# Feed-forward up and down products of a hybrid RWKV-7/S5 layer written out as one ordered pipeline on four queues

## Chip, cores and metric

The kernel runs on one core of a Trainium2 chip. The metric is the device time of one execution in microseconds (us); the time before is the median of three runs. The traces are taken by the hardware profiler from one further execution. PE is TensorE, DVE VectorE, ACT ScalarE, POOL GpSimd, and SP SyncE, which here only issues transfers; ACT issues transfers too.

## The reference, cut to what matters

One layer: RMSNorm, two token mixers in parallel (RWKV-7 and S5), output projection and residual; then the part that is changed here, and a final RMSNorm. Everything is float32.

```python
D_MODEL = 1024; BATCH = 1; SEQ = 1024; DEPTH = 1; D_FF = 4 * D_MODEL
def sq_relu_mlp(x, w_up, w_down):
    return jnp.square(jax.nn.relu(x @ w_up)) @ w_down
...
    x = x + (g_a * y_a + g_b * y_b) @ w_out[l]
    x = x + sq_relu_mlp(rmsnorm(x, norm2_g[l]), w_ff_up[l], w_ff_down[l])
return rmsnorm(x, norm_f_g)
```

## The kernel before

**Precision.** Each float32 operand is split into a high part `hi` (a rounded copy that ACT makes, L123) and a low part `lo = src - hi` (DVE, L117). A product of two operands is three matmuls: hi x hi, hi x lo, lo x hi.

**Strassen.** Both feed-forward matrices are multiplied as 2 x 2 blocks in seven products P1 to P7 (the Winograd form) instead of eight. Each product multiplies a weight block or a sum of weight blocks by a moving block or a sum of moving blocks; `MOV` names the moving one ("11", "21", "22", T1 to T4). Sums of products give the four blocks of the result.

**The up product** (hidden = relu(...)^2, 4096 channels by 1024 tokens) runs in 16 pairs `Pair(j)`, two in each of eight rounds, a (even j) and b (odd j). A pair's product is 12 matmuls of 128 x 512: 4 blocks along the contraction, 3 matmuls each (L1096 to L1098). `w[n]()` returns the split weights of product n; `ready_w` makes them at the first call: P5 needs one sum of weight blocks before (`s1`), P6 three (`s2_`), the others none. The methods P1, P5, P6 run the product and copy its bank out on ACT (tiles `d`, `v5`, `u2`), P2 with C11, P3 and P7 add such a copy to a bank on DVE (`tt`), then `hidden` scales and clips it on DVE (`stt`, L120) and squares it on ACT; P4 does the last two. P1, P6, P7 and P4 of one pair use one bank `x`, P5 and P3 a bank `z`, P2 a bank `y`. Round 0 has the statistics of the second RMSNorm in its midst (`norm_stat`, `norm_out`), which give the scales `rs`.

`moving` then makes the sums T1, T2, T3, T4 of the four hidden blocks on DVE and writes the seven moving blocks to the scratch `tD` in memory, seven issues of 256 KB on ACT's queue (L1208). The w_up weights of a pair come in four loads per round, 512 KB each, on SP's queue (L1066).

**The down product** runs its seven products in the order P1, P5, P6, P7, P3, P2, P4, each over eight units q. `unit(n, q)` loads a 512 KB block of w_dn and a 512 KB block of `tD` (tile `traw`, L1298), forms the weight sum in the kept blocks on DVE, and splits both into `rb` tiles (`rhi`, `rlo`); a unit is 24 matmuls (L1305 to L1307). After a product, DVE adds its four banks to the residual tiles `x2`, loaded within P1. The last two units of P4 are cut into 256-column pieces, with the final norm between them.

**Room.** `gp` has 32 slots of 128 x 512; fourteen of them hold the split moving operands with k = 3 all through the up product, the others rotate for weights and T1, T2, T4. The other split moving operands lie in the pools kxa and kxb (tiles `kx`), which later hold kept weight blocks of the down product. `rb` opens where `gp` closes, 16 slots, of which nine are first taken by unused tiles `rskip`.

**What sets the order.** Every engine runs its own instructions in one order. Only in the last pieces are PE and DVE taken as written (`tc.manual_schedule(engines={E.PE, E.DVE})`); everywhere else the framework's scheduler orders the instructions of each engine from data dependences and modelled times. Transfers signal their landing on eight semaphores in rotation (DMAHW0 to DMAHW7); the next user of a semaphore waits for the transfer that used it before.

## Time and profile before

| quantity | value |
| --- | --- |
| time before, median of 3 | 1618.44 us (1617.98 to 1620.98) |
| profiled execution | 1623.29 us |
| its span, first to last instruction | 1621.5 us |
| PE busy | 94% |
| DVE busy | 66% |
| ACT busy | 45% |
| mean granted clock of TensorE | 0.966 |
| HBM traffic over the span | 142 GB/s |

Times in the profile are in us from the span's start. A row of a timeline gives start, duration, engine (with a q behind it: its queue, issuing a transfer), line, operation, output<-input, shape, count, and in brackets the idle time before and what ended it. L12 is line 12 of the kernel that the row is from. Matmul durations overlap, since matmuls are pipelined: how far starts lie apart is what one costs. The clock is in shares of the full TensorE clock.

### The profile page before, as it was taken

The numbers are of one execution on the slowest core, as the hardware profiler recorded it, in microseconds if no ns is written. First come the engines' busy times: TensorE is split into PE (matmuls) and PEld (weight loads), VectorE is DVE, ScalarE is ACT, GpSimd is POOL, SyncE is SP. The second block draws the span as 40 slices with busy tenths as digits, with TensorE's granted clock in tenths as the row PEclk, the third lists the DMA queues.
The fourth block names the chain that finished last, engine by engine and source line by source line (L and its number), as shares of the span: only waits on it lengthen the run. The fifth ranks groups of instructions, "written<-read, shape, count | busy, mean of one in ns | idle before, by whom it ended". The sixth has DMA issues, their size and how long they took to land.

```text
span 1621.5 us, 22364 instructions
## 1 busy us (share of the span) xinstructions
PE 1529.1 (94%) x8056; PEld 1240.7 (77%) x8056; DVE 1077.0 (66%) x2119; ACT 730.1 (45%) x1259; POOL 80.2 (5%) x107
## 2 busy tenths in 40 slices
PE   7999999999999999999999888889888699999997
PEld 5787787787788778788888776667676578888886
DVE  8668767877576778656666655655655578756564
ACT  7645566765664443234444433323333244333441
POOL 3110001011011010000000000000000000000000
PEclk9999899999999999999999998989989899999998
DMA  7544434245335245741244323332324966532571
GB/s 236 182 146 134 127 105 131 86 143 151 92 117 172 77 132 164 253 124 46 78 149 156 122 102 127 122 138 110 108 100 176 348 222 197 192 104 91 182 245 54
DMA packets 137679, 232.73 MB, mean 144 GB/s; under 512 B 42529, under 2 KB 52897, under 8 KB 137569
## 3 DMA queue, kind: packets, MB, share of 16 engines
q1 hardware_dynamic: 119648, 195.65, 37.7%
q10 hardware_dynamic: 17280, 33.56, 5.4%
q0 software_dynamic: 640, 2.10, 0.6%
q8 instruction: 63, 1.03, 0.3%
q14 instruction: 48, 0.39, 0.1%
HBM read 167.16 MB, written 62.91 MB: 142 GB/s over the span
## 4 chain that ended last, share of the span: by engine, by line
PE 85%; DVE 5%; DMA 4%; ACT 3%; issue 1%; SPq 1%; ACTq 0%; POOL 0%; POOLq 0%; DVEq 0%
PE mm L162 6%; PE mm L160 6%; PE mm L161 6%; PE b L160 4%; PE b L162 4%; PE b L161 4%; PE mm L1096 4%; PE mm L1097 4%; PE mm L1098 4%; PE b L1306 4%; PE b L1307 4%; PE b L1305 3%; PE b L1096 2%; PE b L1097 2%; PE sm L718 2%; PE b L1098 2%
## 5 line engine op out<-in xcount | busy, mean ns | idle before, releaser
L160 PE MATMUL mm<-s,whi 128*128 128x512 f32 x528 | 213.6, 405 | 0.0
L162 PE MATMUL mm<-s,wlo 128*128 128x512 f32 x528 | 213.3, 404 | 0.0
L161 PE MATMUL mm<-s,whi 128*128 128x512 f32 x528 | 210.6, 399 | 0.0
L123 ACT ACTIVATE whi<-wraw 128x512 fp32r<-128x512 f32 x176 | 103.2, 624 | 149.4 <-PE mm L161 54.4
L117 DVE TENSOR_TENSOR wlo<-wraw,whi 128x512 fp32r<-128x512 f32 x176 | 117.0, 685 | 53.5 <-ACT whi L123 53.0
L162 PEld LDWEIGHTS mm<-s,wlo 128*128 128x128 f32 x528 | 100.0, 189 | 24.1 <-issue 4.2
L160 PEld LDWEIGHTS mm<-s,whi 128*128 128x128 f32 x528 | 99.9, 189 | 24.0 <-issue 4.3
L161 PEld LDWEIGHTS mm<-s,whi 128*128 128x128 f32 x528 | 99.9, 189 | 23.0 <-issue 3.6
L123 ACT ACTIVATE row<-row 128x512 f32<-128x512 f32 x64 | 40.4, 631 | 159.6 <-DVE row L120 151.9
L1305 PE MATMUL b<-rhi 128*128 128x512 f32 (+1 forms) x272 | 102.9, 383 | 9.0 <-ACT rhi L123 9.0
L1096 PE MATMUL mm<-kx,gp 128*128 128x512 f32 x192 | 80.7, 420 | 32.6 <-ACT gp L123 32.6
L1306 PE MATMUL b<-rlo,rhi 128*128 128x512 f32 (+1 forms) x272 | 103.9, 382 | 4.2 <-DVE rlo L117 4.2
L1307 PE MATMUL b<-rhi,rlo 128*128 128x512 f32 (+1 forms) x272 | 103.7, 381 | 0.0
L123 ACT ACTIVATE rhi<-kx 128x1024 fp32r<-128x1024 f32 x40 | 42.4, 1059 | 114.4 <-PE b L1306 56.6
L183 POOL TENSOR_TENSOR statm<-statm,cst 128x8 f32<-128x8 f32 (+2 forms) x23 | 35.7, 1550 | 1168.0 <-DVE statm L114 1088.4
L123 ACT ACTIVATE gp<-s 128x512 fp32r<-128x512 f32 x119 | 69.7, 627 | 51.4 <-DVE s L117 30.6
L117 DVE TENSOR_TENSOR rlo<-kx,rhi 128x1024 fp32r<-128x1024 f32 x40 | 48.9, 1223 | 55.9 <-ACT rhi L123 55.9
L117 DVE TENSOR_TENSOR gp<-s,gp 128x512 fp32r<-128x512 f32 x119 | 77.2, 687 | 5.6 <-ACT gp L123 4.9
L1098 PE MATMUL mm<-kx,gp 128*128 128x512 f32 x192 | 78.8, 410 | 1.7 <-DVE gp L117 1.7
L1097 PE MATMUL mm<-kx,gp 128*128 128x512 f32 x192 | 79.1, 412 | 0.0
L117 DVE TENSOR_TENSOR s<-s,s 128x512 f32<-128x512 f32 (+2 forms) x120 | 74.4, 652 | 6.1 <-ACT s L820 4.6
L1096 PEld LDWEIGHTS mm<-kx,gp 128*128 128x128 f32 x192 | 38.5, 201 | 43.6 <-ACT gp L123 35.5
(349 smaller groups left out, 3660.5 us busy)
## 6 DMA issues: line engine op xcount, KB each, us to landing
wraw<-in_w_in SPq DMA_DIRECT2D x136, 256.0 KB
wblk<-in_w_dn SPq DMA_DIRECT2D x40, 512.0 KB
s<-in_w_up SPq DMA_DIRECT2D x32, 512.0 KB
traw<-tDT SPq DMA_DIRECT2D x32, 512.0 KB
tD<-row ACTq DMA_DIRECT2D x48, 256.0 KB
tDT<-gp ACTq DMA_DIRECT2D x48, 256.0 KB
traw<-tD SPq DMA_DIRECT2D x24, 512.0 KB
xraw<-in_xT SPq DMA_DIRECT2D x32, 256.0 KB
```

The costliest lines, as they stand in the source:

```text
L117: V.tensor_tensor(out=out, in0=a, in1=b, op=op)
L123: S.activation(out=out, in_=in_, func=f, **kw)
L160: PE.matmul(out, lhsT=hi[:, a], rhs=rhi(k), start=(k == 0), stop=False)
L161: PE.matmul(out, lhsT=hi[:, a], rhs=rlo(k), start=False, stop=False)
L162: PE.matmul(out, lhsT=lo[:, a], rhs=rhi(k), start=False, stop=(k == nk - 1))
L183: G.tensor_tensor(out=m, in0=m, in1=K("mhalf")[:, 0:nj * n].rearrange("p (a b) -> p a b", b=n), op=ALU.pow)
L1096: PE.matmul(p, lhsT=hi[:, a], rhs=bh, start=(first and k == 0), stop=False, skip_group_check=True)
L1097: PE.matmul(p, lhsT=hi[:, a], rhs=bl, start=False, stop=False, skip_group_check=True)
L1098: r = PE.matmul(p, lhsT=lo[:, a], rhs=bh, start=False, stop=(k == 3), skip_group_check=True)
L1305: PE.matmul(p, lhsT=wh[:, a], rhs=th[:, c], start=first, stop=False, skip_group_check=True)
L1306: PE.matmul(p, lhsT=wh[:, a], rhs=tl[:, c], start=False, stop=False, skip_group_check=True)
L1307: PE.matmul(p, lhsT=wl[:, a], rhs=th[:, c], start=False, stop=last, skip_group_check=True)
```

## The change

From the first up product to the end, PE, DVE, ACT and SP now take their instructions as written. A list `steps` gives the order of the 112 up products. At step i the program writes: the product; its `take` (copy, or sum, scale and square); `prep(i + 5)`, the split of the weights of the product five steps later; and one piece of `later`. `moving` is cut into three such pieces (two sums and three writes; two sums and two writes; two writes), which run at the three steps after aP4 and after bP3. A round's w_up loads are issued at the first step of the round before.

From step 101 on `after_a` loads the operands of the first four down units, into slots of `kx` (now one tag for each slot, so that each tile's slot is known) and `s2` that the last round no longer reads; at step 109 it closes `gp`, opens `rb` with all 16 slots, and splits units 0 and 1 there and at step 111. The last pairs' T1, T2, T4 (j from 14 on) go into halves of freed `kx` slots (`spare_half`). In the down product a step is 24 matmuls, the split of the unit two steps on (`prep_u`), the loads of the one four on (`load_next`) and one piece of `later`, where the takes of the product before now stand in two pieces. `x2` is loaded in the second half of P1. In pair 0 the first P5 sum `s12` uses another tile slot. The last 256-column pieces are as before. No matmul is added or removed.

```diff
+    def kxt(i, dt=F32R):
+        return (kxa if i < 8 else kxb).tile([128, 2, 512], dt, tag=f"kx{i}", name="kx")
...
+        def product(self, n):
+            if n == "P1":
+                self.x = mmtile(ps_mm)
+            elif n == "P5":
+                self.z = mmtile(ps2, "b")
+            elif n == "P2":
+                self.y = st()
+            b = {"P2": "y", "P5": "z", "P3": "z"}.get(n, "x")
+            product(getattr(self, b), self.w, n, n in ("P1", "P5", "P2"))
+        def take(self, n):
+            if n == "P1":
+                self.d = wp.tile([128, 512], F32, tag="wraw", bufs=3, name="d")
+                S.copy(out=self.d, in_=self.x)
+            elif n == "P5":
+                self.v5 = wz.tile([128, 512], F32, tag="z", name="v5")
+                S.copy(out=self.v5, in_=self.z)
+            elif n == "P6":
+                self.u2 = wz.tile([128, 512], F32, tag="zo", name="u2")
+                S.copy(out=self.u2, in_=self.x)
+            elif n == "P4":
+                c = self.row1[:, 0]
+                stt(c, self.x, 0.0, rs[0], ALU.max, M_)
+                act(c, c, AF.Square)
+            else:
+                c, h, add, p = {"P2": (self.row0[:, 0], 0, "d", "y"), "P3": (self.row0[:, 1], 1, "u2", "z"),
+                                "P7": (self.row1[:, 1], 1, "v5", "x")}[n]
+                tt(c, getattr(self, add), getattr(self, p), A_)
+                hidden(c, h)
+        def keep(self, *nt):
+            for n, t in nt:
+                S.dma_start(out=tD[n, self.j // 2][:, self.j % 2], in_=t)
         def moving(self):
             b11, b12, b21, b22 = self.row0[:, 0], self.row0[:, 1], self.row1[:, 0], self.row1[:, 1]
-            t1, t2, t4 = gpt(), gpt(), gpt()
-            tt(t1, b12, b11, B_)
-            tt(t2, b22, t1, B_)
-            tt(b12, b22, b12, B_)
-            tt(t4, b21, t2, B_)
-            for n, t in (("11", b11), ("T1", t1), ("T2", t2), ("22", b22), ("T3", b12), ("21", b21), ("T4", t4)):
-                S.dma_start(out=tD[n, self.j // 2][:, self.j % 2], in_=t)
-    for j in range(0, 16, 2):
-        a, b = Pair(j, None if j else wu[0]), Pair(j + 1, None if j else wu[1])
-        if j == 0:
-            a.P1()
-            a.P2()
-            b.P1()
-            stats = [norm_stat(acc2[h], wz, ps2, "b") for h in range(2)]
-            a.P5()
-            a.P6()
-            b.P5()
-            b.P6()
-            with tc.issue_after(a.p6.ins):
-                for h in range(2):
-                    norm_out(stats[h], rs[h], lambda: wz.tile([128, 512], F32, tag="xacc", bufs=2, name="dup2"),
-                             ps2, "b")
-            a.C11()
-        else:
-            a.P1()
-            a.P5()
-            b.P1()
-            a.P6()
-            b.P5()
-            b.P6()
-            a.P2()
-            a.C11()
-        a.P7()
-        a.P3()
-        b.P7()
-        a.P4()
-        a.moving()
-        b.P2()
-        b.C11()
-        b.P4()
-        b.P3()
-        b.moving()
-    gpc.close()
-    rb = pool("rb", 16, reuse_waits="tile")
-    for _ in range(9):
-        rb.tile([128, 1024], F32R, tag="rb", name="rskip")
-    x2 = {}
+            t1, t2, t4 = (gpt(), gpt(), gpt()) if self.j < 14 else [spare_half() for _ in range(3)]
+            def first():
+                tt(t1, b12, b11, B_)
+                tt(t2, b22, t1, B_)
+                self.keep(("11", b11), ("22", b22), ("21", b21))
+            def second():
+                tt(b12, b22, b12, B_)
+                tt(t4, b21, t2, B_)
+                self.keep(("T1", t1), ("T2", t2))
+            return [first, second, lambda: self.keep(("T3", b12), ("T4", t4))]
...
+    E = mybir.EngineType
+    ctx.enter_context(tc.manual_schedule(engines={E.PE, E.DVE, E.Activation, E.SP}))
...
+    def prep_u(n, q):
+        w, t = raw_u.pop((n, q))
+        a, k = kept_a.get(q), kept_s.get(q)
+        if n == "P1":
...
+        def pair_of(src):
+            return split(src, [rbp[0].tile([128, 1024], F32R, tag="rb", name=x) for x in ("rhi", "rlo")])
+        ready_u[n, q] = pair_of(w), pair_of(t)
+    def after_a(i):
+        if i in (101, 103, 105, 107):
+            load("P1", (i - 101) // 2)
+        if i == 109:
+            gpc.close()
+            rbp.append(pool("rb", 16, reuse_waits="tile"))
+        if i in (109, 111):
+            prep_u("P1", (i - 109) // 2)
+    ROUND = "aP1 aP5 bP1 aP6 bP5 bP6 aP2 aP7 aP3 bP7 aP4 bP2 bP4 bP3".split()
+    FIRST = "aP1 aP2 bP1 aP5 aP6 bP5 bP6 aP7 aP3 bP7 aP4 bP2 bP4 bP3".split()
+    steps = [(2 * r + (o[0] == "b"), o[1:]) for r in range(8) for o in (ROUND if r else FIRST)]
+    pair, later = {}, []
+    def prep(i):
+        if i < len(steps):
+            j, n = steps[i]
+            wu[j][n]()
+    def drain(k):
+        for _ in range(min(k, len(later))):
+            later.pop(0)()
+    prep(2)
+    prep(3)
+    prep(4)
+    ahead = 5
+    for i, (j, n) in enumerate(steps):
+        r, o = divmod(i, 14)
+        if o == 0 and r < 7:
+            for jj in (2 * r + 2, 2 * r + 3):
+                wu[jj] = weights_up(jj)
+        if n == "P1":
+            pair[j] = Pair(j)
+        pair[j].product(n)
+        if i == 1:
+            continue
+        pair[j].take(n)
+        if i == 2:
+            stats = [norm_stat(acc2[h], wz, ps2, "b") for h in range(2)]
+        if i == 5:
+            for h in range(2):
+                norm_out(stats[h], rs[h], lambda: wz.tile([128, 512], F32, tag="xacc", bufs=2, name="dup2"),
+                         ps2, "b")
+            pair[0].take("P2")
+        while ahead < min(i + 6, len(steps)) and (i > 4 or ahead < i + 4):
+            prep(ahead)
+            ahead += 1
+        drain(1)
+        if (j % 2 == 0 and n == "P4") or (j % 2 and n == "P3"):
+            later += pair[j].moving()
+        after_a(i) if i >= 98 else None
+    drain(9)
+    ORDER = ("P1", "P5", "P6", "P7", "P3", "P2", "P4")
...
-    for i, n in enumerate(("P1", "P5", "P6", "P7", "P3", "P2", "P4")):
-        ps = [mmtile(ps2, "b") if i % 2 == 0 else (mmtile(ps_mm) if mp < 2 else st()) for mp in range(4)]
-        for q in range(6 if n == "P4" else 8):
-            u = unit(n, q)
...
+        u = ready_u.pop((n, q))
+        for jp in range(2):
+            for mp in range(4):
+                mm3(ps[mp], u, mp, jp, 0, 512, q + jp == 0, q == 7 and jp == 1)
+        if t + 2 < len(units):
+            prep_u(*units[t + 2])
+        load_next()
+        if n == "P1" and q > 3:
+            for m in (2 * q - 8, 2 * q - 7):
+                x2[m] = s2()
+                SY.dma_start(out=x2[m], in_=xD[m])
+        drain(1)
+        if q == 7:
+            later += [lambda n=n, ps=ps: [take(n, mp, ps[mp]) for mp in (0, 1)],
+                      lambda n=n, ps=ps: [take(n, mp, ps[mp]) for mp in (2, 3)]]
+            if n == "P3":
+                later += rows_out(fa[1], list(range(8)), 1)
+                later.append(lambda: stat1.append(norm_stat(fa[1][0], wz, ps2, "b")))
+                later.append(lambda: stat1.append(norm_out(stat1[0], None, lambda: fa[1][0], ps2, "b")))
+                later += [lambda k=k: [scaled(1, 0, 512, stat1[1], m) for m in range(k, k + 4)] for k in (0, 4)]
+            elif n == "P2":
+                later += rows_out(fa[0], [0, 2, 4, 6], 0)
+    drain(9)
```

What moves, at three places. First DVE in round 4 from the sum of the first pair's P2 on. `d`, `v5`, `u2` are copies of products, `st`, `mm`, `b` banks, `row0` and `row1` hold the hidden blocks, `rs0`, `rs1` the scales; `gp` with two inputs is a low part, or with `row` a moving sum. Before:

```order
L117 TENSOR_TENSOR row0_10097<-d_10122,st_10227 128x512
L120 SCALAR_TENSOR_TENSOR row0_10097<-row0_10097,rs0_88 128x512
L117 TENSOR_TENSOR row1_10098<-v5_10143,mm_10105 128x512
L120 SCALAR_TENSOR_TENSOR row1_10098<-row1_10098,rs1_89 128x512
L117 TENSOR_TENSOR row0_10097<-u2_10183,b_10124 128x512
L120 SCALAR_TENSOR_TENSOR row0_10097<-row0_10097,rs1_89 128x512
L117 TENSOR_TENSOR gp_10322<-row0_10097 128x512
L117 TENSOR_TENSOR row1_10104<-v5_10204,mm_10145 128x512
L117 TENSOR_TENSOR gp_10323<-row1_10098,gp_10322 128x512
L117 TENSOR_TENSOR row0_10097<-row1_10098,row0_10097 128x512
L120 SCALAR_TENSOR_TENSOR row1_10104<-row1_10104,rs1_89 128x512
L120 SCALAR_TENSOR_TENSOR row1_10098<-mm_10105,rs0_88 128x512
```

And now:

```order
L117 TENSOR_TENSOR row0_10127<-d_10142,st_10257 128x512
L120 SCALAR_TENSOR_TENSOR row0_10127<-row0_10127,rs0_88 128x512
L117 TENSOR_TENSOR gp_10274<-s2_9809,gp_10273 128x512
L117 TENSOR_TENSOR row1_10128<-v5_10169,mm_10129 128x512
L120 SCALAR_TENSOR_TENSOR row1_10128<-row1_10128,rs1_89 128x512
L117 TENSOR_TENSOR gp_10293<-s2_9810,gp_10292 128x512
L117 TENSOR_TENSOR row0_10127<-u2_10214,b_10156 128x512
L120 SCALAR_TENSOR_TENSOR row0_10127<-row0_10127,rs1_89 128x512
L117 TENSOR_TENSOR gp_10312<-s2_9809,gp_10311 128x512
L117 TENSOR_TENSOR row1_10180<-v5_10233,mm_10181 128x512
L120 SCALAR_TENSOR_TENSOR row1_10180<-row1_10180,rs1_89 128x512
L117 TENSOR_TENSOR gp_10331<-s2_10119,gp_10330 128x512
```

The low part of a later weight, which needs ACT, now stands between the takes of neighbouring products, and the pair's moving sums stand behind them.

Second, ACT where round 7 begins (row pair 12 and 13 of the hidden blocks is number 6 in `tD`), with each row's waits. `gp` is a weight's high part. Before:

```order
L1208 DMA tDT16_204<-gp_11021 128x512 [waits DMAHW3_49,DVE_49]
L1208 DMA tDT26_212<-gp_11022 128x512 [waits DMAHW4_49,DVE_49]
L123 ACTIVATE gp_11048<-s2_11035 128x512 [waits PE_49]
L1208 DMA tDT36_220<-row0_10731 128x512 [waits DMAHW5_49,DVE_49]
L123 ACTIVATE gp_11069<-s12_11067 128x512 [waits PE_49]
L1208 DMA tDT46_228<-gp_11023 128x512 [waits DMAHW6_49,DVE_49]
L123 ACTIVATE gp_11088<-s2_11041 128x512 [waits PE_49]
L123 ACTIVATE gp_11109<-s12_11067 128x512 [waits DVE_49,PE_49]
L123 ACTIVATE gp_11130<-s12_11128 128x512
L123 ACTIVATE gp_11151<-s12_11128 128x512 [waits DVE_49,PE_49]
L123 ACTIVATE gp_11170<-s2_11035 128x512 [waits PE_49]
L1159 COPY d_11064<-mm_11047 128x512 [waits PE_49]
```

And now:

```order
L1183 DMA tD116_180<-row0_10807 128x512 [waits DMAHW2_49,Activation_49]
L1183 DMA tD226_196<-row1_10808 128x512 [waits DMAHW3_49]
L1183 DMA tD216_188<-row1_10808 128x512 [waits DMAHW4_49,Activation_49]
L1167 COPY v5_11103<-b_11090 128x512 [waits PE_49]
L123 ACTIVATE gp_11105<-s2_10747 128x512
L1183 DMA tDT16_204<-gp_11058 128x512 [waits DMAHW5_49,DVE_49]
L1183 DMA tDT26_212<-gp_11059 128x512 [waits DMAHW6_49,DVE_49]
L1164 COPY d_11128<-mm_11115 128x512 [waits PE_49]
L123 ACTIVATE gp_11130<-s2_10748 128x512
L1183 DMA tDT36_220<-row0_10807 128x512 [waits DMAHW7_49,DVE_49]
L1183 DMA tDT46_228<-gp_11060 128x512 [waits DMAHW1_49,DVE_49]
```

The writes of the pair before now stand between the copies of P1, P5 and P1 of the new round. In the built program DMAHW2 to DMAHW6 at these writes are the semaphores of SP's loads for the first down units (`kx_11154`, `s2_11156`, `kx_11195`, `s2_11197`, `kx_11238`), which wait for bP1 of round 7.

Third, ACT at the passage from the up to the down product. `rhi` is the high part of a down operand. Before:

```order
L1208 DMA tD117_181<-row0_11045 128x512
L123 ACTIVATE row1_11046<-row1_11046 128x512
L1208 DMA tD217_189<-row1_11046 128x512
L123 ACTIVATE row0_11045<-row0_11045 128x512
L1208 DMA tDT17_205<-gp_11335 128x512
L1208 DMA tDT27_213<-gp_11336 128x512
L1208 DMA tDT37_221<-row0_11045 128x512
L1208 DMA tDT47_229<-gp_11337 128x512
L123 ACTIVATE rhi_11370<-kx_11368 128x1024
L123 ACTIVATE rhi_11376<-traw_11374 128x1024
```

And now:

```order
L123 ACTIVATE rhi_11365<-kx_11195 128x1024 [waits PE_49]
L123 ACTIVATE rhi_11369<-s2_11197 128x1024 [waits DMAHW1_49]
L1183 DMA tD117_181<-row0_11113 128x512 [waits DMAHW1_49,Activation_49]
L1183 DMA tD227_197<-row1_11114 128x512 [waits DMAHW2_49]
L1183 DMA tD217_189<-row1_11114 128x512 [waits DMAHW3_49,Activation_49]
L1183 DMA tDT17_205<-kx_11295 128x512 [waits DMAHW7_49,DVE_49]
L1183 DMA tDT27_213<-kx_11364 128x512 [waits DMAHW1_49,DVE_49]
L1183 DMA tDT37_221<-row0_11113 128x512 [waits DMAHW3_49,DVE_49]
L1183 DMA tDT47_229<-kx_11364 128x512 [waits DMAHW5_49,DVE_49]
L123 ACTIVATE rhi_11414<-kx_11238 128x1024
L123 ACTIVATE rhi_11418<-s2_11240 128x1024
```

Unit 1's two high parts stand ahead of the last pair's seven writes, unit 2's behind them; the last write's DMAHW5 is that of an SP load further on (`kx_11566`).

More of the change, by code (lines that the diff above doesn't have):

```diff
@@ L1001, in trunk @@
     run5.close()
-    kxb = pool("kxb", 13, side="right")
+    kxb = pool("kxb", 1, side="right")
     ss = {}
@@ L1106, in trunk @@
         if m == 3:
-            wu = [weights_up(j, load_up(j)) for j in range(2)]
+            wu = {j: weights_up(j) for j in range(2)}
         if m == 7:
@@ L1290, in split2 @@
-    def split2(src):
-        hi, lo = (rb.tile([128, 1024], F32R, tag="rb", name=nm) for nm in ("rhi", "rlo"))
-        return split(src, (hi, lo))
-    def unit(n, q):
-        w = split2(weights_dn(n, q))
-        t = wp.tile([128, 2, 512], F32, tag="whi", name="traw")
-        SY.dma_start(out=t, in_=tD[MOV[n], q])
-        return w, split2(flat(t))
-    def mm3(p, u, mp, jp, c0, c1, first, last):
+            w = wblock("21", q)
+        elif n != "P6":
+            w = wblock({"P7": "21", "P3": "12", "P2": "12", "P4": "22"}[n], q)
@@ L1302, in mm3, with load_next @@
+    drain(9)
+    ORDER = ("P1", "P5", "P6", "P7", "P3", "P2", "P4")
+    units = [(n, q) for n in ORDER for q in range(8)]
+    last, prs, pos = [], [], [4]
+    def load_next():
+        if pos[0] < len(units):
+            load(*units[pos[0]])
+            pos[0] += 1
+    def mm3(p, u, mp, jp, c0, c1, first, stop):
         (wh, wl), (th, tl) = u
@@ L1306, in mm3 @@
         PE.matmul(p, lhsT=wh[:, a], rhs=tl[:, c], start=False, stop=False, skip_group_check=True)
[L1307 removed]
+        PE.matmul(p, lhsT=wl[:, a], rhs=th[:, c], start=False, stop=stop, skip_group_check=True)
     ud = [kx_f32() for _ in range(2)]
@@ L1368, in trunk, with take @@
[L1368 to L1397 removed]
+    def take(n, mp, p):
+        e, o, d = x2[2 * mp], x2[2 * mp + 1], ud[mp // 2][:, mp % 2]
+        if n == "P1":
+            S.copy(out=d, in_=p)
+            tt(e[:, 0], e[:, 0], d, A_)
+        elif n == "P5":
+            tt(e[:, 1], e[:, 1], p, A_)
+            tt(o[:, 1], o[:, 1], p, A_)
+        elif n == "P6":
+            tt(d, d, p, A_)
+            tt(e[:, 1], e[:, 1], d, A_)
+        elif n == "P7":
+            tt(d, d, p, A_)
+            tt(o[:, 1], o[:, 1], d, A_)
+            tt(o[:, 0], o[:, 0], d, A_)
+        else:
+            f = {"P3": 1, "P2": 0}[n]
+            tt(e[:, f], e[:, f], p, A_)
@@ new lines, in rows_out, with some @@
+    def rows_out(fa, ms, h):
+        def some(k):
+            for m in ms[k:k + 4]:
+                sq_acc(fa[0], x2[m][:, h], m == ms[0])
+        fa.append(facc())
+        return [lambda k=k: some(k) for k in range(0, len(ms), 4)]
+    fa = {0: [], 1: []}
+    stat1 = []
+    for t, (n, q) in enumerate(units):
+        i = ORDER.index(n)
+        if q == 0:
+            ps = [mmtile(ps2, "b") if i % 2 == 0 else (mmtile(ps_mm) if mp < 2 else st()) for mp in range(4)]
+        if n == "P4" and q > 5:
+            last.append(ready_u.pop((n, q)))
+            continue
+        u = ready_u.pop((n, q))
[20 more added lines that the diff above has]
+                later += rows_out(fa[0], [0, 2, 4, 6], 0)
@@ new lines, in trunk, with piece @@
+    drain(9)
+    acc = fa[0][0]
+    def piece(mp, c0, c1):
+        c = slice(c0, c1)
+        for qi in range(2):
+            for jp in range(2):
+                mm3(ps[mp][:, c], last[qi], mp, jp, c0, c1, False, qi + jp == 2)
+        y = x2[2 * mp + 1][:, 0, c]
+        tt(y, y, ps[mp][:, c], A_)
+        sq_acc(acc[:, c], y, False)
+    lo, hi = (0, 256), (256, 512)
+    al, ah = acc[:, 0:256], acc[:, 256:512]
+    for mp in range(4):
+        piece(mp, *lo)
+    piece(0, *hi)
+    m0 = norm_stat(al, wz, ps_mm, "mm")
@@ L1400, in _pack_k @@
+    piece(1, *hi)
+    piece(2, *hi)
+    r0 = norm_out(m0, None, lambda: al, ps_mm, "mm")
+    for m in range(4):
+        scaled(0, *lo, r0, m)
+    piece(3, *hi)
+    m1 = norm_stat(ah, wz, ps_mm, "mm")
+    for m in range(4, 8):
+        scaled(0, *lo, r0, m)
+    r1 = norm_out(m1, None, lambda: ah, ps_mm, "mm")
+    for m in range(8):
+        scaled(0, *hi, r1, m)
 def _pack_k(w, nt):
```

191 lines of the change are left out of this document (47 added, 144 removed).

## Prediction

> **What bounds the kernel now.** I read the profile's first two parts, then TensorE's waits, then windows cut at the rounds and at the passage from the up to the down product, and last the engines' timelines in one round.
>
> ```profile
> span 1621.5 us, 22364 instructions
> PE 1529.1 (94%) x8056; PEld 1240.7 (77%) x8056; DVE 1077.0 (66%) x2119; ACT 730.1 (45%) x1259; POOL 80.2 (5%) x107
> PE   7999999999999999999999888889888699999997
> PEclk9999899999999999999999998989989899999998
> ...
> PE mm L1096 <- ACT gp L123: 32.6, 7, 4.7
> PE st L1096 <- ACT gp L123: 19.9, 8, 2.6
> PE b L1305 <- ACT rhi L123: 9.0, 1, 9.0
> PE b L1306 <- DVE rlo L117: 4.2, 1, 4.2
> ```
>
> PE (TensorE) is the bound, and its dips lie in slices 23 to 32: the feed-forward up product and the passage to the down product. In the waits' rows (engine, line, what it waited for: total, times, longest) it waits for the high part of a weight, which ScalarE (ACT) makes at L123: seven and eight times, so twice in each of the eight rounds; and at the first down unit for both parts of its operand. The clock sags in the same slices. So I cut windows at the rounds (the fourth row holds five) and at the passage.
>
> ```profile
> 888.83:942.65 53.82, 44.49 (x194) 35.40 (x192) 36.11 (x58) 21.83 (x39) 2.77 (x2) 0.93 0.36 133
> 942.65:991.26 48.61, 41.48 (x168) 33.47 (x168) 28.31 (x45) 16.26 (x29) 0.00 (x0) 0.92 0.33 120
> 991.26:1041.55 50.29, 43.16 (x169) 34.39 (x169) 28.33 (x45) 16.50 (x29) 0.00 (x0) 0.91 0.31 115
> 1041.55:1284.00 242.45, 210.99 (x840) 169.20 (x840) 135.76 (x212) 80.57 (x138) 0.00 (x0) 0.92 0.40 147
> 1284.00:1292.67 8.67, 0.00 (x0) 0.00 (x0) 5.06 (x7) 2.68 (x4) 0.00 (x0) 0.67 1.03 415
> 1292.67:1320.00 27.33, 23.13 (x86) 18.44 (x87) 23.96 (x21) 12.00 (x12) 0.00 (x0) 0.79 0.89 307
> 1320.00:1600.00 280.00, 280.00 (x1260) 232.68 (x1259) 180.89 (x186) 108.71 (x117) 1.01 (x1) 1.00 0.48 154
> ...
> 1010.33 0.39 PE L1096 MATMUL st<-kx,gp 128*128 128x512 f32 x1
> 1013.05 0.39 PE L1096 MATMUL mm<-kx,gp 128*128 128x512 f32 x1
> ```
>
> The columns are length, busy time of PE, weight load, DVE, ACT and POOL, clock, DMA share and GB/s. The two PE rows are the starts of two neighbouring products: 12 matmuls take 2.72, 0.2267 each. The up product's 112 products would be 304.6 without loss; its rounds, the first four rows, took 395.2: 90.5 lost. The passage lost 8.7, and the 86 matmuls of the first stretch of the down product (19.5) lost 7.8. **Together 107.0.** From 1320 on nothing is lost. VectorE (DVE) has 28.3 of work in a round and ACT 16.5, against 14 x 2.72 = 38.1 for PE: both fit, so the waits come from order.
>
> **The up product, rounds 1 to 6.** The change splits each weight five products ahead and runs takes, splits and sums in written order. The two old waits go with that: a weight's high part stands no longer behind the squares and writes of the pair before it on ACT's queue, but five products ahead of its use. No instruction of the loop is removed; what is late next follows from the takes' own durations.
>
> ```profile
> 1013.25 0.69 DVE L117 TENSOR_TENSOR row<-d,st 128x512 f32<-128x512 f32 x1 [10.13 <-PE st L1098]
> 1013.97 0.69 DVE L120 SCALAR_TENSOR_TENSOR row<-row,rs 128x512 f32<-128x512 f32 x1
> 1014.70 0.63 ACT L123 ACTIVATE row<-row 128x512 f32<-128x512 f32 x1 [3.58 <-DVE row L120]
> 1015.36 0.33 ACTq L1208 DMA_DIRECT2D tD<-row  x1
> 976.81 1.15 ACT L123 ACTIVATE gp<-s 128x512 fp32r<-128x512 f32 x2
> 1001.23 1.89 DVE L117 TENSOR_TENSOR gp<-s,gp 128x512 fp32r<-128x512 f32 x3
> ```
>
> DVE starts 0.20 after a product ends (1013.05 to 1013.25). A DVE instruction that needs the one ahead starts 0.72 after it, one that doesn't 0.60 (three in 1.89). ACT starts 0.04 after DVE's end; an instruction of its own takes 0.63, or 0.52 with another behind it (two in 1.15). A DMA issue takes 0.33. A take of P2, P3 or P7 now runs sum 0.72, scale 0.72, square on ACT 0.53, high part on ACT 0.66 with its handover, low part on DVE 0.60: a ping-pong of 3.24, longer than PE's 2.72, because DVE's next take stands behind the low part, and that behind ACT. From the end of a round's first P2:
>
> - 0.20, and 4 x 3.24 = 12.96 (aP2, aP7, aP3, bP7)
> - aP4: 2.6 (one weight sum, no separate sum before the scale)
> - bP2: 3.24 and two moving sums at 0.66: 4.56
> - bP4: scale 0.72, three weight sums 1.95, low part 0.6, two moving sums: 4.35
> - bP3, up to the end of the copy of the next aP1, which on ACT stands behind square, high part and two DMA issues: 3.92
>
> That is 28.6. PE needs ten products, 27.2, until the next aP6, which overwrites that copy's bank. So **1.4 is lost in each round, 8.4 in six**, against 10.4 to 12.2 before (the third row and a fifth of the fourth, less 38.1). Its bounds are 0, if the handovers are a twentieth shorter, and 3.4, if each of the ten steps is 0.2 longer; I take the rows' own sum. The lateness doesn't carry over: at P1, P5 and P6 DVE has a low part and at most three sums, up to 2.5 against 2.72, so it is level again by the next P2. The weights themselves are ready, since five products, 13.6, lie between split and use. The moving sums' 14 writes of a round are now three groups at three later steps on ACT, 4.7 of issues that lie in its idle share; only the last two of them stand ahead of a copy, and are in the 3.92. SyncE (SP) loads a round's weights one round ahead: cost nothing, hidden by 38 of PE's work.
>
> **Round 0.**
>
> ```profile
> 894.27 1.84 PE L180 MATMUL stat<-cst,acc 128*128 128x1 f32 x16
> 897.21 0.50 PE L1096 MATMUL b<-kx,gp 128*128 128x512 f32 x1 [0.52 <-ACT gp L123]
> 899.63 0.79 PE L1098 MATMUL mm<-kx,gp 128*128 128x512 f32 x1 [1.69 <-DVE gp L117]
> 914.85 1.03 PE L173 MATMUL rsb<-cst,dup 128*128 128x128 f32 x8
> ```
>
> Statistics 1.84 and broadcasts 0.8 stay; of these first splits 2.2 stays; the broadcasts, which PE now meets in written order, wait for ACT's copies, twice 1.4 (an estimate: two ACT instructions at 0.63 and the handovers; bounds 0, as before, and twice 2.5, the longest wait seen for a copy chain here); the half clock 3.4. Sum 11.0, where the first row shows 53.8 - 38.1 = 15.7.
>
> **Half clock.**
>
> ```profile
> 929.27:932.40 3.13, 3.13 (x13) 2.29 (x13) 1.97 (x3) 1.15 (x2) 0.00 (x0) 1.00 0.60 209
> 1026.57:1031.28 4.71, 4.71 (x13) 3.46 (x14) 1.97 (x3) 1.15 (x2) 0.00 (x0) 0.64 0.75 265
> 991.26:994.60 3.34, 3.34 (x8) 2.65 (x9) 3.28 (x7) 1.87 (x4) 0.00 (x0) 0.50 0.55 213
> 929.27 0.50 PE L1096 MATMUL st<-kx,gp 128*128 128x512 f32 x1 [2.48 <-ACT gp L123]
> ```
>
> Both 13-matmul windows follow a 2.5 wait; one ran at 1.00, the other at 0.64. At 0.50 a stretch of 3.4 costs 1.7. So waits of 2.5 bring the half clock sometimes, and I charge none for 1.4, one for round 7's wait, one for the passage and two pieces for round 0. The Trainium skill, "TensorE: Matmul & The Clock Gate", Part 1, says half rate comes after at least one idle free-running window of about 3.4 us; the 0.64 after 2.5 speaks against that as a bare threshold. By the page no wait here is long enough, and 6.8 of the sum would go: that is rival D.
>
> **Round 7.** ACT's writes of the round before carry waits for the landing of SyncE's first loads of down operands, and the copy of bP1 stands behind them on ACT; bP6 needs it. The loads wait for bP1's last reads of their slots.
>
> ```profile
> 1298.92 0.33 SPq L1298 DMA_DIRECT2D traw<-tD  x1
> 1303.91 1.06 ACT L123 ACTIVATE rhi<-traw 128x1024 fp32r<-128x1024 f32 x1 [1.82 <-DMA traw<-tD]
> ```
>
> Before, a 512 KB load took 5.0 from issue to use, of which 1.3 is transfer at the passage's 415 GB/s and 3.7 fixed. Five such loads and four writes of 256 KB, 3.67 MB, are 8.8; with 3.7 and the copy's 0.6 it is 13.1 after bP1 starts, where bP6 wants it at 9.6 (three products and the round's 1.4): 3.5 late, or 6.6 at the 307 GB/s of the stretch behind. The lower bound is none, if the loads land at once on idle queues. I take 4, nearest the 415 row, since in both the engines carry such a burst; with the round's 1.4 and a clock piece 1.7: **7.1**.
>
> **The passage.** The first two units are now loaded and split within round 7; 8.7 and 7.8 become
>
> ```profile
> 1291.58 1.04 ACT L123 ACTIVATE rhi<-traw 128x1024 fp32r<-128x1024 f32 x1
> 1297.67 1.22 DVE L117 TENSOR_TENSOR rlo<-traw,rhi 128x1024 fp32r<-128x1024 f32 x1
> ```
>
> these terms:
>
> - Unit 0's second high part takes a slot that bP4 reads last: 0.2 + 1.04 + two low parts 2.44 + bP4's scale on DVE 0.72 = 4.4 after bP4, of which bP3 covers 2.7: 1.7.
> - Unit 1's high parts stand behind bP3's take: 0.2 + 1.44 + 0.63 + five issues 1.65 + 2.08 + two low parts 2.44 + a moving sum 0.66 = 9.1 after bP3, wanted after the 1.7 and unit 0's 5.44, at 7.1: 2.0.
> - Unit 2's stand behind the last pair's seven writes on ACT, the last of which waits for an SP load: 2.3 of issues and a low part 1.2: 3.5.
>
> Sum 7.2, with a clock piece **8.9**; its bounds are 2.3, one split of each kind, and the old 16.5. From there on a unit has 24 matmuls, 5.4, for two high parts at 1.04 on ACT and two low parts and a weight sum at 1.22 on DVE, split two units ahead: they are hidden, as the row from 1320 shows them now (PE 280.00 of 280.00). The takes of a product move into the next one's first two units, on the same cover. The pieces at the end are as before: cost nothing.
>
> **Sum.** 11.0 + 8.4 + 7.1 + 8.9 = 35.4 instead of 107.0: 71.6 less. The profiled execution (1623.29, its span 1621.5) becomes 1551.7; it lay 4.85 above the median of the runs, so from 1618.44 the time is **1546.8**.
>
> **Rivals.**
>
> - A: the ping-pong is slower than the rows' sum. At 0.2 more a handover the ten steps end 2 later: 3.4 a round and a half-clock piece in each, 7 x 3.7 = 26 more: 1573. For it: the row at 0.64 after 2.5. Against: the rows leave 0.04 between DVE and ACT.
> - B: it is 5% faster, and the rounds lose nothing: 7 x 1.4 = 9.8 less, 1537. For it: an independent DVE pitch is 0.60, and a sum right after a low part may go at that. Against: the scale needs the sum.
> - C: the other side. ACT now serves in one order. A write T1 or T2 that waits for a w_up load holds squares and high parts behind it. SP issues that load at step 3 of a round and ACT reaches the wait at step 12: nine products, 24.5. A round's four loads, 2.1 MB, take 18.2 even at the slowest round's 115 GB/s. Each us past 24.5 is lost in seven rounds, so it turns to a loss at 34.8, and a landing at 36 gives 1547 + 7 x 11.5 = 1627. Transfers would have to be half as fast as in the slowest round.
>
> ```profile
> 1021.60 1.53 ACTq L1208 DMA_DIRECT2D tDT<-gp  x2
> ```
>
> This row is ACT's queue held: 1.53 for two issues of 0.33, the rest a wait for DVE. The same page, in the section on the array's architecture, calls ACT and DVE strict FIFO; the row agrees, and C's price stands without it.
>
> - D: no half-clock pieces, as after 929.27: four pieces of 1.7 less, 1540. Against: the row at 0.50 and the one at 0.64.
> - E: the burst at the passage, at 307 GB/s, with unit 2 and 3 late too, about 17 more: 1564.
> - F: the change doesn't do what it says, the order only moves the same stalls: 1618. Against it: DVE and ACT have 10 and 21 less work in a round than PE.
>
> **How the numbers follow.** Forecast 0.53 (its own range 1540 to 1554, with round 7 and the passage at their nearer bounds), A 0.18, B 0.13, D 0.05, E 0.05, C 0.04, F 0.02. 1530 (B with D) to 1574 (A) leaves out C, F and the mixtures of A with E. Within 0.2%, 3 us, is what a measurement of this kernel can't tell from no change. Faster 0.94, same 0.02 (F), slower 0.04 (C).
>
> **What would show it.** Rounds of 39.5 between the starts of aP1, with one PE wait of about 1.4 at aP6 for ACT's copy of P1; no wait for a high part of a weight; DVE without long idle from aP2 to bP3; a wait of some 4 at bP6 of round 7; three waits in the first three units; nothing after. Wrong would be: any PE wait on weights in steady rounds (prep too late), a clock under 0.95 in rounds 1 to 6 (A), or an ACT DMA issue that holds for more than 2 (C).

## The result and the profile after

The changed kernel takes 1544.1 us (median of 4 runs, 1540.46 to 1549.78), the kernel before 1619.71 (4 runs, 1617.98 to 1625.76): a ratio of 0.953, with a 95% interval of 0.9489 to 0.9571. The forecast was 1546.8 within 1530 to 1574. The profiled execution took 1541.78.

First the head of the page.

```profile
span 1539.9 us, 22347 instructions
PE 1494.1 (97%) x8056; PEld 1216.4 (79%) x8056; DVE 1079.1 (70%) x2119; ACT 730.4 (47%) x1259; POOL 79.3 (5%) x107
PE   7999999999999999999999989999998899999996
PEclk9999999999999999999999999999999999999999
```

Then the largest of what TensorE (PE) waited for from the first up product on, besides the 2.4 of round 0's broadcasts: total, times, longest.

```profile
PE mm L1092 <- ACT d L1164: 10.7, 8, 4.2
PE b L1336 <- DVE rlo L117: 2.7, 3, 0.9
PE mm L1092 <- ACT gp L123: 1.5, 1, 1.5
PE b L1335 <- ACT rhi L123: 1.4, 1, 1.4
```

The two large rows of before, 32.6 and 19.9 for the high part `gp` of a weight, are gone: what is left of that kind is 1.5 in round 0. In their place stands a row that was not there, eight waits for the copy `d` of P1. The clock row, in tenths, no longer sags; the windows below show 0.96 in rounds 0 and 7.

Next the same stages as before, cut at the start of each round (round 0, 1, 2, 3 to 6, 7), then the passage and the rest.

```profile
883.93:931.51 47.58, 43.38 (x193) 35.17 (x192) 29.86 (x48) 21.41 (x38) 2.84 (x2) 0.96 0.29 100
931.51:970.26 38.75, 38.38 (x169) 31.46 (x168) 27.83 (x44) 16.26 (x28) 0.00 (x0) 1.00 0.39 144
970.26:1009.61 39.35, 38.38 (x170) 31.45 (x168) 28.44 (x45) 16.26 (x28) 0.00 (x0) 1.00 0.40 147
1009.61:1167.27 157.66, 153.52 (x674) 125.82 (x672) 113.78 (x177) 65.04 (x112) 0.00 (x0) 1.00 0.37 134
1167.27:1212.78 45.51, 40.28 (x170) 32.51 (x168) 28.58 (x45) 16.56 (x27) 0.00 (x0) 0.96 0.69 263
1212.78:1240.00 27.22, 22.77 (x94) 17.14 (x93) 20.57 (x23) 12.98 (x14) 0.00 (x0) 1.00 0.86 330
1240.00:1518.00 278.00, 278.00 (x1249) 230.95 (x1248) 190.54 (x192) 108.61 (x117) 1.01 (x1) 1.00 0.54 185
```

Against 38.08 for a round without loss, round 0 loses 9.5, rounds 1 to 6 together 7.3, round 7 7.4, and the passage 5.9 (27.22 less 94 matmuls at 0.2267): 30.1, where the kernel before lost 107.0. From the first up product to the end the profiled execution went from 1621.5 - 888.83 = 732.7 to 1539.9 - 883.93 = 656.0, 76.7 less. I call this the stretch and compare kernels by it, because the part ahead of it, which the change does not touch, scatters: its end lay at 883.93 in this execution and at 890.04 in another one of the same kernel, whose stretch was 655.9.

### The profile page after: what moved, and what is told of

The parts are those of the page before. It is cut to its first block, busy times and chain, and to the rows that moved or that the text cites. A ratio compares the mean times of both kernels' runs of the same rounds, so it can differ in the third digit from the quotient of the medians.

```text
span 1539.9 us, 22347 instructions
## 1 busy us (share of the span) xinstructions
PE 1494.1 (97%) x8056; PEld 1216.4 (79%) x8056; DVE 1079.1 (70%) x2119; ACT 730.4 (47%) x1259; POOL 79.3 (5%) x107
## 4 chain that ended last, share of the span: by engine, by line
PE 74%; DVE 11%; DMA 6%; ACT 6%; issue 3%; ACTq 0%; SPq 0%; POOL 0%; DVEq 0%; POOLq 0%
PE mm L162 6%; PE mm L160 6%; PE mm L161 6%; PE b L162 5%; PE b L161 5%; PE b L160 5%; PE b L1336 3%; PE b L1337 3%; PE b L1335 3%; DVE gp L117 2%; DVE row L120 2%; PE mm L1092 2%; PE mm L1094 2%; PE mm L1093 2%; PE sm L718 2%
## 5 line engine op out<-in xcount | busy, mean ns | idle before, releaser
L117 DVE TENSOR_TENSOR gp<-s,gp 128x512 fp32r<-128x512 f32 x119 | 81.5, 690 | 83.8 <-ACT gp L123 83.7
L1092 PE MATMUL mm<-kx,gp 128*128 128x512 f32 x192 | 76.8, 400 | 12.2 <-ACT d L1164 10.7
L123 ACT ACTIVATE gp<-s 128x512 fp32r<-128x512 f32 x119 | 73.9, 627 | 14.6 <-DVE s L117 10.1
L1094 PE MATMUL mm<-kx,gp 128*128 128x512 f32 x192 | 75.7, 394 | 0.2 <-DVE gp L117 0.2
L1093 PE MATMUL mm<-kx,gp 128*128 128x512 f32 x192 | 75.7, 394 | 0.0
L1336 PEld LDWEIGHTS b<-rlo,rhi 128*128 128x128 f32 x272 | 51.2, 188 | 13.0 <-DVE rlo L117 3.8
```

The costliest lines, as they stand in the source:

```text
L117: V.tensor_tensor(out=out, in0=a, in1=b, op=op)
L123: S.activation(out=out, in_=in_, func=f, **kw)
L1092: PE.matmul(p, lhsT=hi[:, a], rhs=bh, start=(first and k == 0), stop=False, skip_group_check=True)
L1093: PE.matmul(p, lhsT=hi[:, a], rhs=bl, start=False, stop=False, skip_group_check=True)
L1094: r = PE.matmul(p, lhsT=lo[:, a], rhs=bh, start=False, stop=(k == 3), skip_group_check=True)
L1336: PE.matmul(p, lhsT=wh[:, a], rhs=tl[:, c], start=False, stop=False, skip_group_check=True)
```

## Experiments

Twelve runs were made, in three groups of four, each group with the kernel before beside it (medians 1624.03, 1622.79 and 1623.66). A stretch is that of one execution, and one half-clock piece more or less moves it by about 1.6 (last section). **Theory 1**: the gain comes from where the split of a weight and the writes of the hidden blocks stand relative to the takes; what is left comes from a ping-pong of VectorE (DVE) with ScalarE (ACT) and from writes on ACT's queue that wait for loads. **Theory 2**, the rival: the written order of the four queues itself brings the gain.

### The framework's order on the changed program

```diff
-    ctx.enter_context(tc.manual_schedule(engines={E.PE, E.DVE, E.Activation, E.SP}))
...
     acc = fa[0][0]
+    ctx.enter_context(tc.manual_schedule(engines={E.PE, E.DVE}))
```

> The changed program (splits five products ahead, loads and slots as changed), but the framework's scheduler orders all four engines up to the last pieces, as in the kernel before. Theory 1, the gain comes from splitting weights well ahead of use, not from the written order: rounds 1 to 6 take 38.1 to 38.6 us without a wait on a weight, since the scheduler need not keep take, split and sum in the ping-pong of the written order; the first down unit waits longer (about 12 us instead of 0.8), because its splits are put behind the last pair's work; the whole about 1540 to 1550 us. Theory 2, the written order on the four queues is what removes the stalls: rounds of 48 to 50 us again, the whole above 1590 us.

It took 1527.77 (ratio 0.9414, 0.9387 to 0.9441), less than the changed kernel. A round, and its last round with the wait at the passage:

```profile
972.88:1010.96 38.08, 38.08 (x170) 31.53 (x168) 28.00 (x45) 16.68 (x28) 0.00 (x0) 1.00 0.42 152
1163.28:1206.89 43.61, 38.24 (x169) 31.34 (x167) 22.26 (x33) 15.02 (x25) 0.00 (x0) 0.98 0.73 267
```

Its PE waits there:

```profile
PE b L1334 <- ACT rhi L123: 5.4, 1, 5.4
PE mm L1094 <- DVE gp L117: 1.9, 1, 1.9
```

PE is busy for all of the 38.08. Theory 2 falls: the written order is not what removed the stalls; against this order it costs 14.8 (stretch 1530.4 - 889.16 = 641.2). My number for the whole was 12 or more too high: I had put 12 on the first down unit, which waited 5.4.

### What removed the stalls: lead and pieces apart

Three more kernels in the framework's order: without the lead, with the moving sums and writes in one piece, and without both.

```diff
 without the lead (and gp closed, rb opened and units 0 and 1 split at step 111):
-        while ahead < min(i + 6, len(steps)) and (i > 4 or ahead < i + 4):
+        while ahead < min(i + 1, len(steps)) and (i > 4 or ahead < i + 4):
 in one piece:
-            later += pair[j].moving()
+            [m() for m in pair[j].moving()]
```

> Framework's order on all engines (as in the run with the changed program in that order), and two things undone: each weight is split in the program only at its product, and a pair's moving sums and seven writes stand in one piece right behind its last take; `gp` closes at the last step. Theory 1, these two make the old stalls, since the scheduler keeps the program's order on ScalarE: the high part of the next round's first weight stands behind bP3's square and the writes that wait for the moving sums (0.2 + 0.72 + 0.72 + 0.63 + 1.4 + 0.7 + 0.6 behind bP3's end): both old waits are back, 2.5 to 2.8 and 4.7 us a round, rounds of 47 to 50 us with the clock near 0.92. Rival, the rest of the change (weights loaded a round ahead, one slot for each tile) is what removed them: rounds stay near 38.1.

> As the run before, but with the moving sums and writes in three pieces at the three following steps, as changed. Theory 1: the first high part no longer stands behind all the writes; the 2.8 us wait goes and the 4.7 us falls to about 2: rounds of 40 to 41 us, clock near 1.0. Rival, lead alone matters: 47 to 50 us.

> Framework's order, weights split five products ahead, moving sums and writes in one piece. Theory 1: the high parts stand ahead of the takes and the writes in the program, so the piece's length no longer matters: rounds of 38.1 us, no wait. Rival, three pieces are needed as they are in the written order: rounds of 40 to 43 us.

| in the framework's order | median, us | ratio | rounds 1 to 6, us | stretch, us |
| --- | --- | --- | --- | --- |
| no lead, one piece | 1610.75 | 0.993 (0.9905 to 0.9955) | 48.64 to 50.34 | 721.0 |
| no lead, three pieces | 1550.67 | 0.9559 (0.9522 to 0.9596) | 40.31 to 41.94 | 662.7 |
| lead of five, one piece | 1531.63 | 0.9438 (0.9408 to 0.9468) | 38.08 | 640.8 |
| lead of five, three pieces | 1527.77 | 0.9414 (0.9387 to 0.9441) | 38.08 | 641.2 |

PE's waits in the first of these:

```profile
PE mm L1092 <- ACT gp L123: 32.6, 7, 4.7
PE st L1092 <- ACT gp L123: 17.3, 7, 2.5
```

And in the second:

```profile
PE b L1092 <- ACT gp L123: 11.6, 7, 1.7
```

Without lead and pieces the old waits are back (before: 32.6 in 7 and 19.9 in 8, here one fewer of the second kind, each as long), so in this order nothing else in the change shortens the rounds. Each of the two alone takes out most of the loss: the lead all of it in rounds 1 to 6, the three pieces about three quarters. With a lead the pieces no longer matter in the framework's order.

### The lead in the written order

```diff
-        while ahead < min(i + 6, len(steps)) and (i > 4 or ahead < i + 4):
+        while ahead < min(i + 3, len(steps)) and (i > 4 or ahead < i + 4):
```

> The weights of a product are split two products ahead instead of five; nothing else is changed. Theory 1, VectorE's ping-pong with ScalarE runs late by several us within a round and only the lead of five products hides it: with a lead of two, TensorE follows the takes (3.24 us instead of 2.72 for P2, P7, P3, bP7, 4.6 and 4.4 for bP2 and bP4), so rounds 1 to 7 take 43 to 45 us instead of 39.35, with waits on high or low parts of weights, and the whole is 1575 to 1585 us. Rival: any lead of more than one product is enough, because splitting takes 1.3 us; rounds stay at 39.4 us and the whole at about 1544 us.

It took 1569.21 (0.9669, 0.9645 to 0.9693), with rounds of 43.94 to 43.99. One of them:

```profile
1020.26:1064.24 43.98, 42.15 (x168) 30.34 (x168) 28.69 (x45) 16.35 (x28) 0.00 (x0) 1.00 0.36 131
```

Its waits for weights:

```profile
PE b L1092 <- ACT gp L123: 9.0, 7, 1.3
PE mm L1092 <- ACT gp L123: 5.3, 8, 1.5
```

The rounds are as theory 1 had them; the whole is 6 under its range. With a lead of two the split that stands behind the take of a product has one product, 2.72, until PE needs it, and a take with its split takes 3.24. With a lead of five it has four products, 10.9. In the changed kernel's round 3 the takes run up to 5.7 late (bP3's begins at 1054.62, the product behind bP3 at 1048.95), and no weight is waited for. In written order the lead is needed.

### The ping-pong

```diff
+        if i > 5 and n in ("P2", "P7", "P3", "P4") and ahead < min(i + 6, len(steps)):
+            prep(ahead)
+            ahead += 1
         pair[j].take(n)
```

This kernel writes the split ahead of the take. Another one has this and issues all of `keep` on SyncE's (SP's) queue; a third, without this edit, undoes the written order of ACT and SP alone. The changed kernel ran beside them.

> The changed kernel itself, for a time on the same chip as the next three. Rounds of 39.35 us, the wait at bP6 of round 7 near 4 us, 1540 to 1552 us. If the scatter of runs lies in the part ahead of the up product, the start of the first up product differs between executions by several us and the rounds do not.

> At the steps of P2, P3, P7 and P4 the split of the later weight is written ahead of the take instead of behind it. Theory 1, the ping-pong: VectorE then needs 2.04 us a step instead of 3.24 and waits for no square; what stays is the copy of the next aP1, which stands on ScalarE behind bP3's square and two writes, so the wait at aP6 falls from about 1.0 to 0.5 or less, the rounds to 38.4 to 38.9, the whole by 3 to 6 us, to about 1539 us. Rival: the 1.0 us is the copy's own latency (end of product, copy, bank release) and not the order: it stays, 39.35 a round.

> As the run before, and all writes of hidden blocks are issued on SyncE's queue instead of ScalarE's. Theory 1: nothing stands ahead of the copies on ScalarE any more, so rounds 1 to 7 take 38.1 to 38.3 us with no wait above 0.2, the wait at bP6 of round 7 is gone, the first units wait under 2 us; 7 x 1.2 and 7 less than the changed kernel, about 1528 us. Rival: SyncE's queue, which now stands at each write until VectorE's sums are there, brings the weights of the next round late: waits on w_up loads in each round, the whole above 1545 us.

> Only TensorE and VectorE in written order; ScalarE and SyncE are ordered by the framework's scheduler. Theory 1, the ping-pong needs the written order on both VectorE and ScalarE: with ScalarE free to make a weight's high part ahead of the square, rounds 1 to 7 take 38.1 us, while the first down unit waits about 8 us for its high part, which the scheduler puts behind the last writes; about 1531 us. Rival: the written order of VectorE alone is what makes the rounds 39.35: they stay there, and the passage is as in the changed kernel, 1544 us.

| kernel | median, us | ratio | rounds 2 to 6, us | stretch, us |
| --- | --- | --- | --- | --- |
| changed kernel again | 1544.71 | 0.9533 (0.9503 to 0.9563) | 39.34 to 39.63 | 655.9 |
| split ahead of take | 1547.97 | 0.9548 (0.9518 to 0.9578) | 38.80 to 38.83 | 657.4 |
| the same, all writes on SP | 1529.02 | 0.9443 (0.9398 to 0.9487) | 38.56 to 38.67 | 640.3 |
| only PE and DVE written | 1529.21 | 0.9434 (0.9409 to 0.946) | 38.07 to 38.09 | 637.6 |

PE's waits for the copy with the split ahead of the take:

```profile
PE mm L1092 <- ACT d L1164: 7.6, 7, 5.0
```

With all writes on SP as well:

```profile
PE mm L1092 <- ACT d L1164: 1.3, 6, 0.3
```

And a round with only PE and DVE written, which has no such wait:

```profile
969.52:1007.61 38.09, 38.09 (x170) 31.54 (x169) 28.41 (x45) 17.14 (x29) 0.00 (x0) 1.00 0.44 159
```

With the split ahead of the take the wait at aP6 falls from 0.97 to 0.43 and the round by 0.55. That is the size expected, but not for the reason expected, which was that DVE would need 2.04 a step. DVE in one of its rounds, the first low part and the starts of three takes from P2's on:

```profile
1035.80 0.69 DVE L117 TENSOR_TENSOR row<-d,st 128x512 f32<-128x512 f32 x1 [0.28 <-PE st L1094]
1038.43 0.69 DVE L117 TENSOR_TENSOR gp<-s,gp 128x512 fp32r<-128x512 f32 x1 [1.22 <-ACT gp L123]
1039.04 0.68 DVE L117 TENSOR_TENSOR row<-v,mm 128x512 f32<-128x512 f32 x1
1042.27 0.68 DVE L117 TENSOR_TENSOR row<-u,b 128x512 f32<-128x512 f32 x1
```

The takes still start 3.24 and 3.23 apart, with the same 1.22 of waiting: the ping-pong is still there. Whichever of take and split comes first in the program, the next high part stands on ACT behind the square of the take before it. What the edit took away is the high part between bP3's square and the copy of aP1 on ACT. The time did not fall: in that execution round 0 took 49.19 at a clock of 0.93 instead of 47.38 at 0.96, the wait at bP6 was 5.0 instead of 4.3, and that for the first unit's low part 2.1 instead of 0.8. With the writes off ACT as well, the wait is 0.2 to 0.3 and the round 38.6, 0.3 more than I had expected, and the takes start 3.24 to 3.29 apart as before. The whole is as expected, and SP's queue does not bring the weights late.

With ACT and SP free the ping-pong itself is gone. DVE's takes of aP7 and aP3 there:

```profile
1029.57 0.69 DVE L117 TENSOR_TENSOR row<-v,mm 128x512 f32<-128x512 f32 x1 [0.71 <-PE mm L1094]
1032.29 0.69 DVE L117 TENSOR_TENSOR row<-u,b 128x512 f32<-128x512 f32 x1 [0.70 <-PE b L1094]
```

They start 2.72 apart and wait for PE, since ACT makes a step's high part ahead of that step's square. DVE as written costs nothing there: the 39.35 needs more than DVE's order. The first unit there waited 2.4 for its high part where I expected 8.

### The writes on ACT's queue

```diff
-                S.dma_start(out=tD[n, self.j // 2][:, self.j % 2], in_=t)
+                (S if self.j < 13 else SY).dma_start(out=tD[n, self.j // 2][:, self.j % 2], in_=t)
```

> The writes of the hidden blocks of the last three pairs (j = 13, 14, 15) are issued on SyncE's queue instead of ScalarE's. Theory 1, the 4.2 us wait at bP6 of round 7 and the waits for the high parts of the third unit come from ScalarE's queue, which stands at writes that wait for the landing of SyncE's loads: the wait at bP6 goes to under 0.5 us, the waits in the first units fall from 4.5 to about 1.7 us in sum, a half-clock stretch may go with them, and the whole is 7 to 9 us shorter, about 1536 us; the rounds before stay at 39.35. Rival: the burst of loads and writes itself is late (bandwidth): the wait at bP6 stays at 3 to 4 us, since as many bytes move, and the time stays at 1544 us.

It took 1537.09 (0.9461, 0.943 to 0.9493), with a stretch of 646.3, 9.6 less than the changed kernel's. Its round 7:

```profile
1171.45:1210.80 39.35, 38.38 (x170) 31.45 (x168) 29.32 (x45) 16.18 (x27) 0.00 (x0) 1.00 0.60 226
```

And ACT in round 7 of the changed kernel (ACTq is its queue, issuing a transfer):

```profile
1177.22 4.89 ACTq L1183 DMA_DIRECT2D tD<-row  x3
1182.16 0.59 ACT L1167 COPY v<-b 128x512 f32<-128x512 f32 x1 [4.37 <-DMA kx<-in_w_dn]
1183.68 2.21 ACTq L1183 DMA_DIRECT2D tDT<-gp  x2
1185.93 0.59 ACT L1164 COPY d<-mm 128x512 f32<-128x512 f32 x1 [2.65 <-DMA kx<-in_w_dn]
```

Three issues of 0.33 took 4.89 and two took 2.21, and both copies behind them wait for a load of down weights that they do not read. With the writes elsewhere round 7 is as long as the others, and the waits in the first units fall from 4.5 to 1.1. The same bytes move. They move later, since the loads on SP's queue now stand behind the writes (the first starts 15.4 behind the round's start instead of 6.3), so this run alone does not tell the queue from the timing of the burst. The two copies do: each stood behind issues that were held until a load landed.

### The early loads

```diff
-        if i in (101, 103, 105, 107):
-            load("P1", (i - 101) // 2)
-        if i == 109:
+        if i == 111:
+            drain(9)
+            for q in range(4):
+                load("P1", q)
...
-        if i in (109, 111):
-            prep_u("P1", (i - 109) // 2)
+            prep_u("P1", 0)
+            prep_u("P1", 1)
```

> Loads and splits of the first four down units are written behind the up product's last step instead of in its last round. Theory 1, the early loads and splits fill the passage: the first unit then waits 8 to 10 us for its splits, which stand behind the last pair's takes and writes, while the third unit no longer waits; the passage loses about 10 instead of 5.5 us and the whole is 4 to 5 us longer, about 1549 us. Rival: the loads too start only there, so a landing is added: 14 to 18 us in the passage, as in the kernel before, the whole about 1555 us.

It took 1549.94 (0.9552, 0.9524 to 0.9581), with a stretch of 661.5, 5.5 longer. The first unit waits 8.3 for its high part and 0.7 for its low part, and the wait at bP6 stays at 3.8. The first load's issue:

```profile
1171.52 0.33 SPq L1225 DMA_DIRECT2D kx<-in_w_dn  x1
```

That is 6.3 behind the start of round 7, as in the changed kernel (1173.58 there). So the loads hang on their slots, not on their place in the program. The early splits are worth about 5 in these two executions; the intervals of the two ratios overlap.

### The version that follows

PE and DVE as written, ACT and SP by the framework, and the last three pairs' writes on SP's queue.

> TensorE and VectorE in written order, ScalarE and SyncE by the framework, and the writes of the last three pairs on SyncE's queue. Theory 1: rounds of 38.1 us, no wait in round 7, and at the passage the first unit's high part no longer stands behind the last writes: 0.6 us there instead of 3.4; from the first up product to the end 634 to 636 us instead of 637.6, the whole about 1526 us, the shortest so far by what a window can show. Rival: the first high part is placed late by the scheduler for other reasons, and the wait of 2.4 stays.

It took 1517.69 (0.9361, 0.9322 to 0.94), 8 under what I expected; its stretch, 633.2, is 1 under. All its waits from the first up product to the third unit:

```profile
PE mm L1092 <- ACT gp L123: 1.5, 1, 1.5
PE b L1335 <- DVE row L117: 0.3, 1, 0.3
PE mm L1094 <- DVE gp L117: 0.2, 1, 0.2
```

Its round 7:

```profile
1163.93:1202.01 38.08, 38.08 (x170) 31.53 (x168) 26.07 (x39) 15.31 (x26) 0.00 (x0) 1.00 0.73 253
```

## Why the prediction was right

**Rounds 1 to 6.** Forecast 1.4 a round and 8.4 in six; measured 7.3 in six, with rounds 2 to 5 at 39.35 (1.27 lost in each) and one wait in each for the copy of P1. DVE in the changed kernel's round 3, from the take of P2 on, shows the ping-pong as summed (the first low part, the start of each take but bP4's, and last ACT's copy for the next aP1; rows between are left out):

```profile
1030.12 0.69 DVE L117 TENSOR_TENSOR row<-d,st 128x512 f32<-128x512 f32 x1 [0.88 <-PE st L1094]
1032.75 0.69 DVE L117 TENSOR_TENSOR gp<-s,gp 128x512 fp32r<-128x512 f32 x1 [1.22 <-ACT gp L123]
1033.36 0.68 DVE L117 TENSOR_TENSOR row<-v,mm 128x512 f32<-128x512 f32 x1
1036.59 0.68 DVE L117 TENSOR_TENSOR row<-u,b 128x512 f32<-128x512 f32 x1
1039.83 0.68 DVE L117 TENSOR_TENSOR row<-v,mm 128x512 f32<-128x512 f32 x1
1043.06 0.68 DVE L120 SCALAR_TENSOR_TENSOR row<-mm,rs 128x512 f32<-128x512 f32 x1
1045.73 0.68 DVE L117 TENSOR_TENSOR row<-d,st 128x512 f32<-128x512 f32 x1
1054.62 0.68 DVE L117 TENSOR_TENSOR row<-u,b 128x512 f32<-128x512 f32 x1
1057.60 0.59 ACT L1164 COPY d<-mm 128x512 f32<-128x512 f32 x1 [0.25 <-issue]
```

PE at aP6 of round 2:

```profile
979.56 0.50 PE L1092 MATMUL mm<-kx,gp 128*128 128x512 f32 x1 [0.97 <-ACT d L1164]
```

Takes start 3.24, 3.23, 3.24 and 3.23 apart, each low part after 1.22 of waiting for ACT. The rest of the chain came as summed, too: aP4 took 2.67 for 2.6, bP2 and bP4 together 8.89 for 8.91, bP3 up to the end of the copy 3.57 for 3.92, in all 28.3 for 28.6. The pieces listed for bP4 add up to 4.59 and not to the 4.35 used (two moving sums at 0.66, as for bP2); the trace has 4.33 (1050.29 to 1054.62), since DVE goes on 0.60 after the scale. Where ACT was free the ping-pong and the wait both went; where the split stood ahead of the take the ping-pong stayed, and only what stood ahead of the copy grew shorter. The forecast's cover of 13.6 for a split is four products, 10.9, since the split stands behind the take; no weight was late by it.

**Round 0.** Forecast 11.0, measured 9.5: the broadcasts waited 1.25 and 1.19 for 1.4 each, and the half clock (0.96 over 47.58) cost less than the two pieces charged.

**Round 7.** Forecast 7.1, measured 7.4, with 4.19 at bP6 where I took 4. The cause was the one forecast, as ACT's rows in round 7 and the run with the writes on SP's queue show.

**The passage.** Forecast 8.9, measured 5.9: the term that was off most. Unit 0 and 1 waited 1.1 and 0.9 for the forecast 1.7 and 2.0; unit 2 waited 2.4 for 3.5; and no half clock came (1.00), where I had charged a piece.

**The sum.** 30.1 is lost where 35.4 was forecast; the stretch became 76.7 shorter where the sum was 71.6. The medians differ by 75.6.

**The rivals.** A needed waits of 3.4 a round and a clock under 0.95: rounds 1 to 6 had 1.00. B, no wait, did not come in this kernel, but is what the framework's order gave. C's block of ACT's queue by a load never came in rounds 1 to 6 (the longest single issue there took 1.19, and PE lost nothing by it); the wait of round 7 is of its kind. D is half right: no piece in the passage, one each in round 0 and round 7. Its ground that no wait would be long enough passed over the 4 forecast for round 7. E did not come: the passage lost 5.9. F fell.

**What the forecast had not seen.** It named the lead as what removes the two old waits, and that held. That the cut of the moving sums into three pieces alone does about three quarters of it, and that the framework's order on the same program has no ping-pong and is 14.8 faster, stands nowhere in it; B had the rounds without loss as a faster ping-pong, not as one that another order avoids.

## What to carry to other kernels

Write a split or any other preparation in the program well ahead of the take it would otherwise stand behind; a long piece of sums and writes goes behind it, or is cut. Where two engines take turns, changing places within a step does not help as long as one engine's next part still stands behind its last; the timeline's rows show whether the step has become shorter. Take such a change apart before fixing the order of all queues by hand: here the structure gave the gain, and the fixed order of ACT and DVE together took a part back. A queue that also computes should issue no transfer whose semaphore another queue's load holds.
